# Blocks of 8 of a triangular inverse on VectorE, through DRAM there and back, in a hybrid recurrent layer

## The chip, the cores and the metric

One Trainium2 chip, one of its cores. The metric is the device time of one execution in microseconds (us), as the median of several runs. A core has TensorE (the page calls its products PE and its weight loads PEld), VectorE (DVE), ScalarE (ACT), GpSimd (POOL) and SyncE (SP), which here issues nearly all DMAs.

## What is computed

One layer that serves two groups of tokens: a prompt of 256 and eight sequences of 8 new tokens, 320 columns in all. In float32:

```python
h = rms_norm(x, norm_g)
p = einsum('nld,dp->nlp', h, w_in)          # one projection, 2048 -> 12416 columns
# branch A, 16 heads of 64: r, k, v, decay w, a from p (token shift, small LoRAs), kk = k normed
#   S_t = S_{t-1} diag(w_t) - (S_{t-1} kk_t)(kk_t * a_t)^T + v_t k_t^T ;  y_t = S_t r_t
# branch B, 8 heads of 128: a gated linear recurrence, S_t = diag(g_t) S_{t-1} + k_t v_t^T
merged = (sigmoid(p[..., OFF_GA:OFF_GB]) * (y_a @ proj_a)
          + sigmoid(p[..., OFF_GB:]) * (y_b @ proj_b))
y = x + merged @ w_out                      # then a last rms_norm; the states are outputs too
```

Branch A is computed in chunks of 64 tokens. Within a chunk the delta rule's update needs the inverse of a unit lower triangular matrix I + N of 64 x 64, one for each head and chunk, where N holds masked products of the keys. For the eight short sequences, N falls apart into blocks of 8.

## The kernel before, in words

All large products are made from float32r halves: each operand is split into a high part (a cast by ScalarE) and the rest (a subtraction by VectorE), and three products (high x high, high x low, low x high) are summed. hhi and hlo hold h, whi and wlo a block of 8 x 128 rows of weights, raw the loaded block (three buffers of each). One tile of 128 output columns takes 2 blocks, 48 products over 320 columns, in a PSUM tile mps.

Three stages:

- The start norms and transposes x, and makes the constants.
- The recorded stage. `record_all` writes down, for each of 8 head pairs p, the eight projection tiles r, k, v, za, q, f, i, zb, and then the recurrences `rwkv` (two heads of branch A) and `hgrn` (one head of branch B). After the pairs it records NFILL = 4 tiles of the gate ga. The calls go into a `Recorder`, which keeps each with an estimated cost and latency. `order()` plans all five engines with these: at each point it takes the operation whose inputs are due, by the longest path behind it, and fills TensorE with the projection's products (the "stream") where nothing else is due. The plan is then issued, so each engine's order is fixed, SP's too. Every instruction so issued has line 1447 in the profile. For operations that read another engine's result, TensorE's plan adds a margin of 250 ns. A DMA on SP is planned at 380 ns, and what needs it at 5500 ns more.
- The output stages. For each of 16 tiles m: the gates ga (made here unless m < NFILL) and gb, the products with proj_a and proj_b (ppa, ppb, lines 359 to 361), the merge (lines 1486 to 1494). Then the product with w_out (lines 1534 to 1540), and the last norm.

In `rwkv`, the part that the change touches runs like this. The masked products are in g2 (in the profile: g). nd (in the profile by its buffer, big) collects the prompt's N for the four chunks and two heads; TensorE transposes it, and ScalarE copies the result into M (buffer uE). The inverse Y is built by doubling: blocks of 2 are I - N by POOL and VectorE, from id64; then for sz = 2, 4, 8, 16, 32 the blocks of sz are joined to blocks of 2 sz by Y21 = -Y22 N21 Y11: a product with M (into a PSUM tile, pP), a masked copy into pp, a product with the transpose xt of Y (buffer uB; pD), and a subtraction into yz. yz holds Y with zeros between the two heads' halves, yd the same without; from the second level on yd is transposed by TensorE to make xt. ys is the inverse for the short sequences, which is done after sz = 4. Products of these operands are in plain float32, each as two instructions on TensorE.

The chain of a pair goes on from yz through four chunks (rhs, uv, st), the output y, a norm over heads (uE, uB), to ya, the pair's part of branch A's output. Most buffers are single: the exponential into uE of a pair follows the product into ya of the pair before.

Of the kernel before, what the change touches and what calls it, by code (L numbers as in the profile page):

```python
# [19 lines left out]
NT = NP_ + NS  # L20
# [18 lines left out]
EXP_LN_SET = 6  # L39

NFILL = 4
BUFS = {"r": 1, "k": 1, "v": 1, "za": 2, "q": 2, "f": 2, "i": 1, "zb": 1}


# [24 lines left out]
class Recorder:  # L69
# [15 lines left out]
    def add(self, eng, name, fn, args, kw):  # L85
# [8 lines left out]
        for j, x in enumerate(aps):  # L94
            t_ = x.tensor
            if "DRam" in type(t_).__name__:
                continue
            key = (t_.name, x.offset, tuple(map(tuple, x.ap)))
            if key not in self.spans:
                self.spans[key] = span_of(x)  # L100
            o.uses.append((*self.spans[key], j == 0, "PSUM" in str(x.space)))
# [193 lines left out]
def hybrid_step(ctx, tc, x_prompt, x_sample, state_rwkv, state_hgrn, state_shift, norm_g, w_in,  # L295
# [68 lines left out]
    def run(gen):  # L364
        for _ in gen:
            pass
# [9 lines left out]
    with tc.tile_pool(name="start", bufs=1) as st, \  # L376
# [53 lines left out]
        fetch(2, 0, 0)  # L430


        id64 = ctile([128, 64], "id64")
# [11 lines left out]
        lvs = st.tile([128, 5, 32], F32, name="lvs")  # L445
        lvz = ctile([128, 5, 2, 32], "lvz")
        seqm = ctile([128, NSEQ], "seqm")
        mk_lv = {}
        V.memset(lvs[low_], 1.0)
        G.memset(seqm[low_], 1.0)  # L450
        for n, sz in enumerate((2, 4, 8, 16, 32)):
            mk_lv[sz] = lvz[:, n]
            lv = lvs[low_, n].rearrange("p (b s) -> p b s", s=sz)
            nb = 32 // sz
            keep_ge(lv, [[-2 * sz, nb], [0, sz]], 0, 1)
            keep_ge(lv, [[2 * sz, nb], [0, sz]], sz - 1, -1)
# [267 lines left out]
             "w1": 384, "w2": 320, "w3": 320, "ks": 128, "ket": 256, "o": NT}  # L724


    CLEAR = {"uB", "uE", "ys", "rhs", "rhs2", "k3", "vm", "w1", "vt", "att", "attc", "az", "rz"}

    def at(name, shape=(128, NT), tag=None, bufs=1, dt=F32):
        tag = tag or name  # L730
# [48 lines left out]
    def rwkv(p, r, k, vp, za):  # L779
# [142 lines left out]
        two = lambda t_, x: t_.rearrange("p a (b two) -> p a b two", two=2)[:, :, :, x]  # L922
        two4 = lambda t_, x: t_.rearrange("p a h (b two) -> p a h b two", two=2)[:, :, :, :, x]
        ys = at("ys", (128, 2, 64))
        idx = [two(id64[:, None], j).to_broadcast([128, 5, 32]) for j in range(2)]
        V.tensor_mul(two(xt[:, 0:5], 0), two(xt[:, 0:5], 0), idx[1])
        V.tensor_sub(two(xt[:, 0:5], 0), idx[0], two(xt[:, 0:5], 0))
        G.tensor_copy(two(xt[:, 0:5], 1), idx[1])
        for c_ in range(2):
            y = yz[HS[c_], :, c_]  # L930
            src = two4(g2[HS[c_], c_:4:2, 0], 1)
            ix = [two(id64[HS[c_], None], j)[:, None].to_broadcast([64, 2, 2, 32]) for j in range(2)]
            G.tensor_mul(two4(y, 1), src, ix[0])
            G.tensor_sub(two4(y, 1), ix[1], two4(y, 1))
            G.tensor_copy(two4(y, 0), ix[0])
            G.tensor_copy(yd[HS[c_]], y)
        ix = [two(id64[0:64, None], j).to_broadcast([64, 2, 32]) for j in range(2)]
        G.tensor_mul(two(ys[0:64], 1), two(g2[0:64, 4, 0], 1), ix[0])
        G.tensor_sub(two(ys[0:64], 1), ix[1], two(ys[0:64], 1))
        G.tensor_copy(two(ys[0:64], 0), ix[0])  # L940


        bk = at("bk", (128, 5, 128))
# [8 lines left out]

        for sz in (2, 4, 8, 16, 32):
            smp = sz < 8
            if sz > 2:
                xt = at("xt", (128, 6, 64), tag="uB")
                px = aps("pX")
                for cp in range(2):  # L960
                    T.transpose(px[:, 128 * cp:128 * cp + 128], yd[:, cp].rearrange("p h t -> p (h t)"), ident)
                if smp:
                    T.transpose(px[:, 256:384], ys.rearrange("p h t -> p (h t)"), ident)
                n = 5 if smp else 4
                S.copy(xt[:, 0:n].rearrange("p c t -> p (c t)"), px[:, :64 * n])
            ahead = lambda t_: t_.rearrange("p (x two s) -> p x two s", two=2, s=sz)[:, :, 1, :]
            n = 5 if smp else 4
# [4 lines left out]
            if smp:  # L972
                T.matmul(ps[:, 256:320], M[:, 2].rearrange("p h t -> p (h t)"), ahead(ys.rearrange("p h t -> p (h t)")),
                         start=True, stop=True)
            pp = at("pp", (128, 5, 64))
            V.tensor_mul(pp[:, :n], ps[:, :64 * n].rearrange("p (c x) -> p c x", x=64),
                         mk_lv[sz].rearrange("p h t -> p (h t)")[:, None].to_broadcast([128, n, 64]))
# [4 lines left out]
            if smp:  # L982
                T.matmul(ps[:, 256:320], xt[:, 4:6, :].rearrange("p c t -> p (c t)"), pp[:, 4], start=True, stop=True)
# [6 lines left out]
            if smp:  # L990
                yv = ys[0:64].rearrange("p h (b two s) -> p (h b) two s", two=2, s=sz)[:, :, 1, :]
                V.tensor_sub(yv, yv, ps[0:64, 256:320].rearrange("p (x s) -> p x s", s=sz))

        bp = parts(bon)
        pbn = aps("pbn")
# [391 lines left out]
    def record_all():  # L1387
# [275 lines left out]
```

## Time and profile before

| | |
|---|---|
| runs | 1119.71, 1120.02, 1121.02 us; median 1120.02 |
| the profiled execution | span 1119.8 us; no other time of it is shown |
| TensorE busy | 1104.9 us, 9244 products |
| VectorE, ScalarE, GpSimd busy | 762.0, 694.2, 187.1 us |
| chain that ended last | TensorE 96% |
| recorded stage | 28.4 to 684.45 us |
| DMA | 159.89 MB, mean 143 GB/s |

Busy time counts an instruction from its start to its end. TensorE's instructions overlap, so a group's sum of lengths is longer than the time that it takes of TensorE; the time from one start to the next is what counts. "A <- B: x, n, y" in the waits says that A waited x us in total, n times, y at the longest, until B was done. Tiles go by their buffers' names: a stands for any PSUM tile of branch A, b for branch B's.

### The profile page before, as it was taken

What the parts mean: (1) busy time and instruction counts of PE and PEld (TensorE: products, weight loads), DVE (VectorE), ACT (ScalarE), POOL (GpSimd) and SP (SyncE); (2) the same over time, 40 slices, a digit from 0 to 9 for tenths busy, and PEclk for the clock granted to TensorE, in tenths of its full rate; (3) what the DMA queues carried; (4) which work ended last, traced back from release to release, by engine and by line L of the source; (5) the groups of instructions that cost most, each with busy time, mean ns of one, the idle gap of its engine ahead of it and who ended that gap; (6) DMA issues with size and microseconds to landing.
All of it is one profiled execution on the core that took longest, in us unless ns stands there. A gap on an engine that the chain in (4) does not pass through costs nothing.

```text
span 1119.8 us, 23680 instructions
## 1 busy us (share of the span) xinstructions
PE 1104.9 (99%) x9244; PEld 1068.4 (95%) x9244; DVE 762.0 (68%) x1631; ACT 694.2 (62%) x1578; POOL 187.1 (17%) x401
## 2 busy tenths in 40 slices
PE   7999999999999999999999999999999999999997
PEld 6999999999999999999999999999999999998886
DVE  8778888887888887887887876444444444437532
ACT  7677777777777778677776876444444444435422
POOL 7531231221311411412322200000000000000000
PEclk9999999999999999999999999999999999999999
DMA  6744545435436435445354345555555555586602
GB/s 193 194 125 117 153 116 148 138 99 155 123 91 165 127 102 165 134 114 156 113 136 133 107 136 148 146 147 152 149 148 152 149 152 150 151 274 227 201 32 95
DMA packets 283189, 159.89 MB, mean 143 GB/s; under 512 B 22909, under 2 KB 273280, under 8 KB 282500
## 3 DMA queue, kind: packets, MB, share of 16 engines
q1 hardware_dynamic: 282708, 157.06, 49.1%
q8 instruction: 73, 1.20, 0.5%
q10 hardware_dynamic: 368, 1.31, 0.3%
q14 instruction: 40, 0.33, 0.1%
HBM read 148.53 MB, written 9.81 MB: 141 GB/s over the span
## 4 chain that ended last, share of the span: by engine, by line
PE 96%; ACT 2%; DMA 1%; issue 0%; DVE 0%; SPq 0%; DVEq 0%; ACTq 0%
PE mps L1447 42%; PE a L1447 10%; PE mps L361 6%; PE mps L359 6%; PE mps L360 6%; PE b L1447 3%; PE po L1536 3%; PE po L1535 3%; PE po L1534 3%; PE ppb L359 2%; PE ppa L359 2%; PE ppa L361 2%; PE ppb L361 2%; PE ppb L360 2%; PE ppa L360 2%; PE y L1447 1%
## 5 line engine op out<-in xcount | busy, mean ns | idle before, releaser
L1447 PE MATMUL mps<-hhi,whi 128*128 128x320 f32 x1088 | 345.1, 317 | 0.0
L1447 PE MATMUL mps<-hlo,whi 128*128 128x320 f32 x1088 | 344.6, 317 | 0.0
L1447 PE MATMUL mps<-hhi,wlo 128*128 128x320 f32 x1088 | 344.0, 316 | 0.0
L1447 PEld LDWEIGHTS mps<-hhi,whi 128*128 128x128 f32 x1088 | 205.0, 188 | 3.6 <-issue 2.7
L1447 PEld LDWEIGHTS mps<-hlo,whi 128*128 128x128 f32 x1088 | 205.1, 189 | 1.1 <-issue 0.4
L1447 PEld LDWEIGHTS mps<-hhi,wlo 128*128 128x128 f32 x1088 | 205.0, 188 | 0.7
L349 ACT CAST whi<-raw 128x1024 fp32r<-128x1024 f32 x88 | 92.4, 1050 | 162.7 <-PE mps L360 107.3
L350 DVE TENSOR_TENSOR wlo<-raw,whi 128x1024 fp32r<-128x1024 f32 x88 | 107.9, 1226 | 125.0 <-ACT whi L349 124.8
L1447 DVE TENSOR_TENSOR wlo<-raw,whi 128x1024 fp32r<-128x1024 f32 x134 | 164.7, 1229 | 17.9 <-ACT whi L1447 16.7
L1447 ACT CAST whi<-raw 128x1024 fp32r<-128x1024 f32 x134 | 140.2, 1046 | 57.6 <-PE mps L1447 56.5
L361 PE MATMUL mps<-hhi,wlo 128*128 128x320 f32 x448 | 138.7, 310 | 0.0
L360 PE MATMUL mps<-hlo,whi 128*128 128x320 f32 x448 | 138.7, 309 | 0.0
L359 PE MATMUL mps<-hhi,whi 128*128 128x320 f32 x448 | 138.6, 309 | 0.0
L359 PEld LDWEIGHTS mps<-hhi,whi 128*128 128x128 f32 x448 | 84.1, 188 | 0.0
L360 PEld LDWEIGHTS mps<-hlo,whi 128*128 128x128 f32 x448 | 84.1, 188 | 0.0
L361 PEld LDWEIGHTS mps<-hhi,wlo 128*128 128x128 f32 x448 | 84.1, 188 | 0.0
L1523 DVE TENSOR_TENSOR wlo<-raw,whi 128x1024 fp32r<-128x1024 f32 x32 | 38.5, 1221 | 37.2 <-ACT whi L1522 36.9
L1522 ACT CAST whi<-raw 128x1024 fp32r<-128x1024 f32 x32 | 32.9, 1050 | 48.1 <-DMA raw<-in_w_out_dram 25.5
L1447 POOL TENSOR_TENSOR vm<-v,seq 96x512 fp32r<-96x512 f32 x16 | 16.8, 1051 | 200.2 <-ACT uK L1447 130.0
L1536 PE MATMUL po<-wlo,mhi 128*128 128x512 f32 x128 | 50.2, 392 | 0.0
L1535 PE MATMUL po<-whi,mlo 128*128 128x512 f32 x128 | 50.1, 391 | 0.0
L1534 PE MATMUL po<-whi,mhi 128*128 128x512 f32 x128 | 50.1, 391 | 0.0
(442 smaller groups left out, 2245.8 us busy)
## 6 DMA issues: line engine op xcount, KB each, us to landing
raw<-in_w_in_dram SPq DMA_DIRECT2D x194, 512.0 KB
raw<-in_w_out_dram SPq DMA_DIRECT2D x32, 512.0 KB
raw<-in_proj_a_dram SPq DMA_DIRECT2D x16, 512.0 KB
raw<-in_proj_b_dram SPq DMA_DIRECT2D x16, 512.0 KB
s<-in_state_hgrn_dram SPq DMA_DIRECT2D x8, 512.0 KB
out_dram<-s SPq DMA_DIRECT2D x8, 512.0 KB
s<-in_state_rwkv_dram SPq DMA_DIRECT2D x8, 256.0 KB
out_dram<-s SPq DMA_DIRECT2D x8, 256.0 KB
```

The costliest lines, as they stand in the source:

```text
L349: S.copy(hi[:, ks], raw[:, ks])
L350: sub.tensor_sub(lo[:, ks], raw[:, ks], hi[:, ks].bitcast(F32))
L359: T.matmul(dst, hi[:, q, :], xhi[:, k, :], start=(k == 0), stop=False)
L360: T.matmul(dst, hi[:, q, :], xlo[:, k, :], start=False, stop=False)
L361: T.matmul(dst, lo[:, q, :], xhi[:, k, :], start=False, stop=(k == nk - 1))
L1447: o.fn(*o.args, **o.kw)
L1522: S.copy(hi, raw)
L1523: V.tensor_sub(lo, raw, hi.bitcast(F32))
L1534: T.matmul(pt, h, hi, start=first, stop=False)
L1535: T.matmul(pt, l, hi, start=False, stop=False)
L1536: T.matmul(pt, h, lo, start=False, stop=end)
```

## The change

Levels 2 and 4 of the doubling go. The diagonal blocks of 8 x 8 of N (64 of the prompt's four chunks and two heads, 16 of the short sequences, and 16 of padding) are gathered into a tile dn (POOL masks, VectorE sums over the blocks of a row), written to a DRAM tile scratch[0] as 768 rows of 8 elements, and read back as nb with one block in each of 96 partitions. There VectorE makes their inverses in y8 by nine small operations: first the 2 x 2 corrections, then the 4 x 4 one. y8 goes to scratch[1] and comes back as ye in the first layout; POOL spreads it to yd and ys, and ScalarE copies yd into yz. All four DMAs are on SP. The planner takes 2600 ns for the latency of DMAs with these DRAM tiles.

Three more gate tiles (m = 4 to 6) are made at the end of the recorded stage, in free buffers of za, q and f; they are stored to DRAM and loaded again in the output loop.

```diff
+NLATE = 3
...
             if "DRam" in type(t_).__name__:
+                if t_.name.startswith("scr"):
+                    o.uses.append((t_.name, 0, 1, 1, j == 0, False))
                 continue
...
-            o.cost, o.lat = 380, 5500
+            o.cost, o.lat = 380, 2600 if any(u[0].startswith("scr") for u in o.uses) else 5500
...
+        id8 = ctile([128, 64], "id8")
+        G.memset(id8, 0.0)
+        G.memset(id8[:, 0:64:9], 1.0)
...
-        for n, sz in enumerate((2, 4, 8, 16, 32)):
+        for n, sz in enumerate((8, 16, 32)):
...
-        M = at("M", (128, 3, 2, 64), tag="uE")
+        M = at("M", (128, 2, 2, 64), tag="uE")
...
-        T.transpose(ps[:, 256:384], g2[:, 4, 0].rearrange("p h t -> p (h t)"), ident)
-        xt = at("xt", (128, 6, 64), tag="uB")
-        S.copy(xt[:, 0:5].rearrange("p c t -> p (c t)"), ps[:, :320])
         for h in range(2):
             for c_ in range(2):
-                S.copy(M[HS[c_], 0:2, h], xt[HS[h], c_:4:2])
-            S.copy(M[0:64, 2, h], xt[HS[h], 4])
+                S.copy(M[HS[c_], :, h], ps[HS[h], :256].rearrange("p (a c s) -> p a c s", c=2, s=64)[:, :, c_])
+
+        lows = at("lows", (128, 4, 8, 8), tag="pp")
+        each = lambda n: seqm[:, None, :, None].to_broadcast([128, n, 8, 8])
+        G.tensor_mul(lows, nd.rearrange("p a h (b j) -> p (a h) b j", j=8), each(4))
+        dn = at("dn", (128, 6, 8))
+        V.tensor_reduce(dn[:, 0:4], lows.rearrange("p c b j -> p c j b"), axis=mybir.AxisListType.X, op=ALU.add)
+        V.tensor_reduce(dn[0:64, 4:6], g2[0:64, 4, 0].rearrange("p h (b j) -> p h j b", j=8),
+                        axis=mybir.AxisListType.X, op=ALU.add)
+        there = lambda t_: t_.rearrange("(c p) j -> p c j", c=6)
+        whole = lambda t_: t_.rearrange("(q i) j -> q (i j)", i=8)
+        Y.dma_start(there(scratch[0]), dn)
+        nb = at("nb", (96, 64), tag="pp")
+        Y.dma_start(nb, whole(scratch[0]))
+        y8 = at("y8", (96, 64))
+        V.tensor_sub(y8, id8[:96], nb)
+        t8 = nb
+        four = lambda o_, *d: bass.AP(y8.tensor, y8.offset + o_, [y8.ap[0], *d])
+        t4 = t8[:, 0:4].rearrange("p (a i) -> p a i", i=2)
+        V.tensor_mul(t4, four(2, [36, 2], [8, 2]), four(19, [36, 2], [0, 2]))
+        V.tensor_add(four(3, [36, 2], [8, 2]), four(3, [36, 2], [8, 2]), t4)
+        V.tensor_mul(t4, four(10, [36, 2], [1, 2]), four(1, [36, 2], [0, 2]))
+        V.tensor_add(four(2, [36, 2], [1, 2]), four(2, [36, 2], [1, 2]), t4)
+        t64 = t8.rearrange("p (i j k) -> p i j k", j=4, k=4)
+        p16 = at("p16", (96, 4, 4))
+        V.tensor_mul(t64, four(4, [8, 4], [0, 4], [1, 4]), four(36, [0, 4], [1, 4], [8, 4]))
+        V.tensor_reduce(p16, t64, axis=mybir.AxisListType.X, op=ALU.add)
+        V.tensor_mul(t64, four(0, [8, 4], [0, 4], [1, 4]),
+                     p16.rearrange("p k j -> p j k")[:, None].to_broadcast([96, 4, 4, 4]))
+        V.tensor_reduce(four(4, [8, 4], [1, 4]), t64, axis=mybir.AxisListType.X, op=ALU.add)
+        Y.dma_start(whole(scratch[1]), y8)
+        ye = at("ye", (128, 6, 8))
+        Y.dma_start(ye, there(scratch[1]))
+
         ys = at("ys", (128, 2, 64))
-        idx = [two(id64[:, None], j).to_broadcast([128, 5, 32]) for j in range(2)]
-        V.tensor_mul(two(xt[:, 0:5], 0), two(xt[:, 0:5], 0), idx[1])
-        V.tensor_sub(two(xt[:, 0:5], 0), idx[0], two(xt[:, 0:5], 0))
-        G.tensor_copy(two(xt[:, 0:5], 1), idx[1])
...
+        wide = lambda t_: t_.rearrange("p h (b j) -> p h b j", j=8)
+        spread = lambda x, n: ye[x, 4 * (n == 2):4 * (n == 2) + n, None, :].to_broadcast([x.stop - x.start, n, 8, 8])
+        G.tensor_mul(yd.rearrange("p a h (b j) -> p (a h) b j", j=8), spread(slice(0, 128), 4), each(4))
+        G.tensor_mul(wide(ys[0:64]), spread(slice(0, 64), 2), each(2)[0:64])
         for c_ in range(2):
+            S.copy(yz[HS[c_], :, c_], yd[HS[c_]])
...
-        for sz in (2, 4, 8, 16, 32):
-            smp = sz < 8
-            if sz > 2:
+        for sz in (8, 16, 32):
...
             ps = aps("pP")
             for cp in range(2):
                 T.matmul(ps[:, 128 * cp:128 * cp + 128], M[:, cp].rearrange("p h t -> p (h t)"),
                          ahead(yz[:, cp].rearrange("p c h t -> p (c h t)")), start=True, stop=True)
-            if smp:
-                T.matmul(ps[:, 256:320], M[:, 2].rearrange("p h t -> p (h t)"), ahead(ys.rearrange("p h t -> p (h t)")),
-                         start=True, stop=True)
...
+    scr = ctx.enter_context(tc.tile_pool(name="scr", bufs=1, space=bass.MemoryType.DRAM))
+    scratch = [scr.tile([768, 8], F32, name=f"scr{j}", tag=f"scr{j}") for j in range(2)]
+    late = [scr.tile([128, NT], F32, name=f"scrg{m}", tag=f"scrg{m}") for m in range(NLATE)]
...
+        for m, (pool, key) in enumerate(((at, "za"), (bt, "q"), (bt, "f"))[:NLATE]):
+            def post(ps, m=m, pool=pool, key=key):
+                t_ = pool(key, (128, NT), bufs=BUFS[key])
+                sigm(t_, ps)
+                Y.dma_start(late[m], t_)
+            tile_of(OFF_GA + 128 * (NFILL + m), post)
...
             ga = fpr.tile([128, NT], F32, name="ga", tag="ga", bufs=2)
-            run(main(OFF_GA + 128 * m, lambda ps: sigm(ga, ps)))
+            if m < NFILL + NLATE:
+                nc.sync.dma_start(ga, late[m - NFILL])
+            else:
+                run(main(OFF_GA + 128 * m, lambda ps: sigm(ga, ps)))
```

More of the change, by code (lines that the diff above doesn't have):

```diff
@@ L430, in hybrid_step @@
         fetch(2, 0, 0)
-        id64 = ctile([128, 64], "id64")
+        id64 = st.tile([128, 64], F32, name="id64")
         G.tensor_add(id64, ident[:, 0:64], ident[:, 64:128])
@@ L444, in hybrid_step @@
         low_ = HS[0]
-        lvs = st.tile([128, 5, 32], F32, name="lvs")
-        lvz = ctile([128, 5, 2, 32], "lvz")
+        lvs = st.tile([128, 3, 32], F32, name="lvs")
+        lvz = ctile([128, 3, 2, 32], "lvz")
         seqm = ctile([128, NSEQ], "seqm")
@@ L724, in hybrid_step @@
              "w1": 384, "w2": 320, "w3": 320, "ks": 128, "ket": 256, "o": NT}
-    CLEAR = {"uB", "uE", "ys", "rhs", "rhs2", "k3", "vm", "w1", "vt", "att", "attc", "az", "rz"}
+    CLEAR = {"uB", "uE", "ys", "dn", "rhs", "rhs2", "k3", "vm", "w1", "vt", "att", "attc", "az", "rz"}
     def at(name, shape=(128, NT), tag=None, bufs=1, dt=F32):
@@ L923, in rwkv @@
-        two4 = lambda t_, x: t_.rearrange("p a h (b two) -> p a h b two", two=2)[:, :, :, :, x]
+                S.copy(M[HS[c_], :, h], ps[HS[h], :256].rearrange("p (a c s) -> p a c s", c=2, s=64)[:, :, c_])
[4 more added lines that the diff above has]
+        V.tensor_reduce(dn[:, 0:4], lows.rearrange("p c b j -> p c j b"), axis=mybir.AxisListType.X, op=ALU.add)
@@ L929, in rwkv @@
+        G.tensor_mul(yd.rearrange("p a h (b j) -> p (a h) b j", j=8), spread(slice(0, 128), 4), each(4))
+        G.tensor_mul(wide(ys[0:64]), spread(slice(0, 64), 2), each(2)[0:64])
         for c_ in range(2):
[L930 to L940, printed above, removed]
+            S.copy(yz[HS[c_], :, c_], yd[HS[c_]])
         bk = at("bk", (128, 5, 128))
@@ L950, in rwkv @@
         S.copy(bk[:, 4], ps[:, :128])
-        for sz in (2, 4, 8, 16, 32):
-            smp = sz < 8
-            if sz > 2:
[L958 to L961, printed above, removed]
-                if smp:
-                    T.transpose(px[:, 256:384], ys.rearrange("p h t -> p (h t)"), ident)
-                n = 5 if smp else 4
-                S.copy(xt[:, 0:n].rearrange("p c t -> p (c t)"), px[:, :64 * n])
+        for sz in (8, 16, 32):
+            xt = at("xt", (128, 4, 64), tag="uB")
+            px = aps("pX")
+            for cp in range(2):
+                T.transpose(px[:, 128 * cp:128 * cp + 128], yd[:, cp].rearrange("p h t -> p (h t)"), ident)
+            S.copy(xt.rearrange("p c t -> p (c t)"), px[:, :256])
             ahead = lambda t_: t_.rearrange("p (x two s) -> p x two s", two=2, s=sz)[:, :, 1, :]
-            n = 5 if smp else 4
             ps = aps("pP")
@@ L971, in rwkv @@
                          ahead(yz[:, cp].rearrange("p c h t -> p (c h t)")), start=True, stop=True)
-            if smp:
-                T.matmul(ps[:, 256:320], M[:, 2].rearrange("p h t -> p (h t)"), ahead(ys.rearrange("p h t -> p (h t)")),
-                         start=True, stop=True)
-            pp = at("pp", (128, 5, 64))
-            V.tensor_mul(pp[:, :n], ps[:, :64 * n].rearrange("p (c x) -> p c x", x=64),
-                         mk_lv[sz].rearrange("p h t -> p (h t)")[:, None].to_broadcast([128, n, 64]))
+            pp = at("pp", (128, 4, 64))
+            V.tensor_mul(pp, ps[:, :256].rearrange("p (c x) -> p c x", x=64),
+                         mk_lv[sz].rearrange("p h t -> p (h t)")[:, None].to_broadcast([128, 4, 64]))
             ps = aps("pD")
@@ L981, in rwkv @@
                          pp[:, 2 * cp:2 * cp + 2].rearrange("p c x -> p (c x)"), start=True, stop=True)
-            if smp:
-                T.matmul(ps[:, 256:320], xt[:, 4:6, :].rearrange("p c t -> p (c t)"), pp[:, 4], start=True, stop=True)
             for c_ in range(2):
@@ L989, in rwkv @@
                     S.copy(yd[HS[c_]].rearrange("p a h (b two s) -> p a (h b) two s", two=2, s=sz)[:, :, :, 1, :], y)
-            if smp:
-                yv = ys[0:64].rearrange("p h (b two s) -> p (h b) two s", two=2, s=sz)[:, :, 1, :]
-                V.tensor_sub(yv, yv, ps[0:64, 256:320].rearrange("p (x s) -> p x s", s=sz))
         bp = parts(bon)
```

1 line of the change is left out of this document (removed).

## The prediction

> **What bounds the kernel now.** I read the page's busy times first, then the stretches, then the waits. The first two lines of the fence are from the page, the next two from the stretches, cut where the recorded stage ends (684.45 us; columns: length, then the busy time of PE, PEld, DVE, ACT and POOL, granted clock, DMA share, GB/s); the last two are from the waits, with the total, the number and the longest.
>
> ```profile
> span 1119.8 us, 23680 instructions
> PE 1104.9 (99%) x9244; PEld 1068.4 (95%) x9244; DVE 762.0 (68%) x1631; ACT 694.2 (62%) x1578; POOL 187.1 (17%) x401
> 28.40:684.45 656.05, 655.22 (x6461) 641.20 (x6460) 540.59 (x1335) 489.08 (x1260) 165.46 (x353) 1.00 0.48 133
> 684.45:975.00 290.55, 290.55 (x1984) 290.55 (x1983) 131.49 (x160) 130.74 (x196) 0.00 (x0) 1.00 0.53 151
> PE a L1447 <- DVE pp L1447: 0.7, 2, 0.3
> ACT whi L1447 <- PE mps L1447: 56.5, 47, 2.7
> ```
>
> TensorE is never out of work: in the recorded stage it is busy for 655.2 of 656.1 us, at the full granted clock, and it waits 0.7 us there in all. So both stages last as long as TensorE's instructions. An instruction taken away saves the time from its start to the next start, if its place isn't taken by a wait. VectorE is busy for 82% of that stage (540.59 of 656.05), ScalarE for 75%.
>
> **What the change removes.** Per head pair, TensorE loses the third transpose into M, all of levels 2 and 4 (three products, three corrections each), and level 4's three transposes back. Pair 2's timeline of TensorE has them (start, length, how many). Lengths overlap, so I take starts.
>
> ```profile
> 225.64 0.38 PE L1447 MATMUL a<-ident,big 128*128 128x128 f32 x2
> 225.85 0.27 PE L1447 MATMUL a<-ident,g 128*128 128x128 f32 x1
> 225.88 0.39 PE L1447 MATMUL mps<-hhi,wlo 128*128 128x320 f32 x1
> 226.11 0.31 PE L1447 MATMUL mps<-hhi,whi 128*128 128x320 f32 x1
> 226.26 0.31 PE L1447 MATMUL mps<-hlo,whi 128*128 128x320 f32 x1
> ...
> 228.72 0.61 PE L1447 MATMUL a<-yz,uE 128*128 128x128 f32 x4
> 229.09 0.39 PE L1447 MATMUL mps<-hhi,wlo 128*128 128x320 f32 x1
> 229.32 0.33 PE L1447 MATMUL a<-ys,uE 128*128 128x64 f32 x2
> 229.46 0.39 PE L1447 MATMUL mps<-hhi,whi 128*128 128x320 f32 x1
> 229.69 0.31 PE L1447 MATMUL mps<-hlo,whi 128*128 128x320 f32 x1
> ...
> 236.76 0.78 PE L1447 MATMUL a<-pp,uB 128*128 128x128 f32 x6
> 237.35 0.39 PE L1447 MATMUL mps<-hlo,whi 128*128 128x320 f32 x1
> 237.58 0.31 PE L1447 MATMUL mps<-hhi,wlo 128*128 128x320 f32 x1
> ...
> 238.61 0.61 PE L1447 MATMUL a<-yz,uE 128*128 128x128 f32 x4
> ```
>
> A stream product (mps) takes 0.147 us from start to start (226.11 to 226.26, rounded). Three transposes: 226.11 - 225.64 - 0.147 = 0.32, or 0.11 each. A level's products: 229.69 - 228.72 less two stream products = 0.68. Its corrections: 237.58 - 236.76 - 0.147 = 0.67. Per pair: 0.11 + 2 x (0.68 + 0.67) + 3 x 0.11 = 3.14 us. Eight pairs: **25.1 us**.
>
> **What it moves.** Three gate tiles of 48 products go from the output stage into the recorded one. Two rows of the output loop's multiply by the gate, of tiles whose gate is made before it and of the others (first and last start at the end), give the price:
>
> ```profile
> L1486 DVE TENSOR_TENSOR mt<-ga,ppa x12: 486/489/489, 758.4 to 990.7; 128x320 f32<-128x320 f32 x12
> L1486 DVE TENSOR_TENSOR mt<-sga,ppa x4: 487/489/489, 695.0 to 737.3; 128x320 f32<-128x320 f32 x4
> ```
>
> (990.7 - 758.4) / 11 = 21.1 us against (737.3 - 695.0) / 3 = 14.1: a gate tile is 7.0 us of TensorE, 48 x 0.147, in either stage. Sum 0: 21.1 leave one stage and enter the other. Their three stores and three loads of 160 KB stand on SP; the loads ahead of the gb weights, three blocks before TensorE needs those, so I cost them at 0. The cover is that prefetch: without it, a late weight block would show in the output loop as a TensorE wait, of which the second stretch has none. ScalarE's nine exponentials and logarithms move along with the tiles, into ScalarE's free quarter.
>
> **What it adds.** No TensorE work, but a longer chain from the masked products g to the third level: copies, a POOL product and two VectorE sums, four DMAs that each wait for the one before or for VectorE, nine small VectorE operations, a POOL product, two ScalarE copies. Prices from the groups by shape (count | busy us, mean ns), and from ScalarE's timeline (first row):
>
> ```profile
> 224.47 0.82 ACT L1447 COPY big<-g 64x256 f32<-64x256 f32 x2
> L1447 POOL TENSOR_TENSOR fd<-id,fq 128x256 fp32r<-128x256 f32 x16 | 12.1, 758 | 7.6 <-DVE fq L1447 5.1 <-PE a L1447 2.2
> L1447 DVE TENSOR_TENSOR pp<-a,lvz 128x256 f32<-128x256 f32 x24 | 10.2, 425 | 2.6 <-PE a L1447 2.2
> L1447 DVE TENSOR_TENSOR rhs<-a,uK 64x64 f32<-64x64 f32 x48 | 10.6, 221 | 3.8 <-PE a L1447 3.1
> L1447 DVE TENSOR_TENSOR fq<-f,fh 32x8 fp32r<-32x8 f32 x32 | 8.3, 260 | 0.7
> ```
>
> Copies 0.82 + POOL 0.76 + two sums at 0.43 + subtraction 0.22 + four tiny ones at 0.26 + four of 64 elements at 0.22 + POOL 0.76 + copies 0.82 = 6.2 us, and four trips. VectorE's part is 3.0 us a pair, and it loses ten operations, two of them 128x320 products and two over xt, so I count it as no busier; its free 18% covers an error there. POOL loses twelve operations a pair and gains three.
>
> A trip has no row of its own. Its bounds are two cases of 32 KB. The first two rows are stretches around a store issued at 506.87 (SP's row follows): the DMA engines are idle until 508.10 and move it by 508.60, so a trip is not under 1.7 us. The last four are weights of 32 KB that queue behind 512 KB loads at the start: SP issues them, and the casts that wait for them (the releaser is in brackets) start 41.43 - 36.09 = 5.3 and 42.42 - 37.83 = 4.6 us later.
>
> ```profile
> 506.80:508.10 1.30, 1.30 (x12) 1.30 (x11) 0.45 (x2) 0.85 (x4) 0.00 (x0) 1.00 0.00 1
> 508.10:508.60 0.50, 0.50 (x8) 0.50 (x6) 0.21 (x2) 0.50 (x3) 0.00 (x0) 1.00 0.31 66
> 506.87 0.65 SPq L1447 DMA_DIRECT2D out_dram<-so  x1
> 36.09 1.64 SPq L1447 DMA_DIRECT2D w2a<-in_rwkv_w_dram  x1
> 37.83 0.55 SPq L1447 DMA_DIRECT2D w2a<-in_rwkv_a_dram  x1
> 41.43 0.30 ACT L1447 CAST wst<-w2a 64x128 fp32r<-64x128 f32 x1 [0.16 <-DMA w2a<-in_rwkv_w_dram]
> 42.42 0.30 ACT L1447 CAST ast<-w2a 64x128 fp32r<-64x128 f32 x1 [0.69 <-DMA w2a<-in_rwkv_a_dram]
> ```
>
> The DMA engines are 0.48 busy in this stage, so about half of the trips meet a load. At 1.7 us for one half and midway to 4.6 (3.2) for the other, plus 0.3 for the completion (my estimate), a trip is 2.7 us; I take the low end's neighbourhood since a trip issues while SP holds the following loads back. The order written out by the planner counts 0.38 + 2.6 = 2.98. That is what matters: every engine runs the planner's order, so a trip that lands earlier gains nothing, and one that lands later holds TensorE at the third level's product, past the 0.25 us that the planner leaves, and holds behind it the stream and, on SP, the weight loads. SP's own hold is hidden: ScalarE's casts wait for TensorE to free buffers (56.5 us, 47 times), not for loads. A quarter of the trips would meet the first half of a load and land up to 4.6 - 2.98 = 1.6 us late. I count that as one late trip of the four in a pair, by 0.7 us, less 0.25: 0.45 x 8 = **3.6 us**.
>
> The Trainium skill's page "DMA: Bandwidth & Descriptors" (section "Anatomy of one DMA") gives about 2.0 us fixed for one DMA issued by GpSimd, most of it the receipt of the write. The idle 1.3 us in the row above, ahead of any data, says that here much of it lies before the data. By the page no trip would exceed the plan, and the sum would be 1094.7.
>
> **Is the chain too long?** Pair after pair, the exponential into uE waits for the product into ya of the pair before. Their rows (first and last start) and the last piece of the chain that ended last before the stage's end:
>
> ```profile
> L1447 ACT ACTIVATE uE<-uB x8: 456/458/476, 44.1 to 603.2; 128x320 f32<-128x320 f32 x8
> L1447 DVE TENSOR_TENSOR ya<-uE,uA x8: 476/483/493, 128.2 to 677.3; 128x320 f32<-128x320 f32 x8
> 674.63 9.82 PE mps L1447 x67
> ```
>
> The last pair takes 677.3 - 603.2 = 74.1 us. From the copies at 224.47 to the third level at 238.61 are 14.1 us now; 6.2 + 4 x 2.98 = 18.1 after, so a chain is 78.1. TensorE's pace is (677.3 - 128.2) / 7 = 78.4 now and 75.3 after. The chain falls behind by 2.8 us a pair, 22 over eight. It has 684.45 - 677.8 (the last ya's end) = 6.7 us to spare, and the three gate tiles add 21.1 of work that doesn't need it: 27.8. So the lag is hidden. The tiles matter for this alone; without them some 16 us would come back as a wait.
>
> **Sum.** 1119.8 - 25.1 + 0 + 3.6 = 1098.3. The profiled execution's span is 0.2 under the median of the runs shown (1120.02), so the forecast is **1098.5 us**.
>
> **Rivals.**
> 1. Trips late throughout. With landings of 3.2 to 3.7 us, each of 32 costs 0.2 to 0.7 over the plan: 1119.8 - 25.1 + 6 to 22 = 1101 to 1117, middle 1109. For it: the 4.6 and 5.3 above. Against: those stood behind three 512 KB loads.
> 2. Slower: the same place, TensorE's wait at the third level, from 2.98 + 25.1 / 32 = 3.76 us a trip on. At 4.6 it is 32 x 1.62 = 52 us lost, 1146. For it: SP is one queue in order, and the weights' packets stand ahead of the small ones. Against: 0.48 busy, not 1.
> 3. The 32-byte rows. The first store and the last load of a pair move 768 rows each. The 32 KB store's 128 rows pass within the 0.5 us stretch. If rows set the time, 768 take up to 6 x 0.5 = 3.0 us, and such a trip up to 1.3 + 3.0 + 0.3 = 4.6, 1.6 over the plan; at half of that, for two trips a pair, 16 x 0.8 = 13 us, 1108. The same page ("Specifications") says that a transfer under 512 B costs a read and a write back. No row here shows one of 32 B; that would act on the store alone, 8 x 0.8 = 6 us, 1101.
> 4. Nothing comes of it: freed TensorE time turns into waits of the same length, trips of 3.7 to 3.8 us, 1118 to 1122.
>
> **How the numbers follow.** Chances: the forecast (1092 to 1104) 0.52, rival 1 0.15, rival 3 0.09 (0.03 of it by the page's rule, at 1101), rival 4 0.06, slower 0.18. Faster by over 0.2% (2.2 us, what a measurement can tell) is 0.76, same 0.06, slower 0.18. The range, from the sum without any wait, less 2.5 for slots measured in one pair, past rival 1's end: 1092 to 1119; it leaves out the slower cases and most of rival 4.
>
> **What would show it.** Right: the pairs' pace between ya products at 75 to 76 us; TensorE's waits in the stage at 3 to 8 us, most for yz or yd by way of POOL, ScalarE or a DMA; the stage ending near 681; ya of the last pair before it; tiles 4 to 6 of the output loop 14.1 us apart. Wrong: waits over 20 us behind DMAs into nb or ye, SP's longest waits there, a pace of 78 or more, or an idle TensorE at the stage's end.

## The result, and the profile after

The changed kernel takes **1105.1 us** (median; 1102.3 to 1106.5) against 1120.2 us for the kernel before in the same session: a ratio of 0.986, 95% interval 0.9846 to 0.9874. The forecast was 1098.5 us in a range of 1092 to 1119. So it is faster, as forecast, by 15.1 us instead of 21.5.

The profiled execution of the changed kernel took 1104.5 us with a span of 1102.8: some 1.7 us lie outside a span. The span of 1119.8 shown for the kernel before therefore belongs to an execution of about 1121.5, a little above its median, and the two spans overstate the gain by some 1.9 us. That 1119.8 came out near the median, from which the forecast was counted, is chance. In this part the recorded stage's line is 1465 (1447 before, a few lines off in the kernels of the experiments), and the output loop's product with the gate is line 1507 (1486 before). The page of the changed kernel:

```profile
span 1102.8 us, 23134 instructions
PE 1081.3 (98%) x9020; PEld 1043.5 (95%) x9020; DVE 750.6 (68%) x1639; ACT 680.1 (62%) x1530; POOL 154.6 (14%) x328
```

TensorE lost 23.6 us of busy time, near the 25.1 forecast, but its idle time, span less busy, rose from 14.9 to 21.5 us. Where that lies is seen in the stretches (length, then the busy time of PE, PEld, DVE, ACT and POOL, the granted clock, DMA share, GB/s) and in TensorE's waits (total, number, longest):

```profile
28.40:683.95 655.55, 650.01 (x6363) 635.32 (x6362) 529.88 (x1336) 476.71 (x1209) 135.96 (x281) 1.00 0.50 139
...
691.95:695.00 3.05, 1.78 (x8) 1.02 (x8) 2.37 (x4) 2.88 (x5) 0.00 (x0) 1.00 0.89 266
695.00:698.40 3.40, 3.40 (x16) 3.40 (x15) 2.61 (x5) 2.95 (x7) 0.00 (x0) 0.52 0.56 161
```

```profile
PE b L1465 <- issue: 1.9, 1, 1.9
...
PE a L1465 <- DVE yz L1465: 1.2, 2, 0.6
PE a L1465 <- POOL yd L1465: 1.0, 1, 1.0
PE mps L362 <- ACT whi L352: 1.0, 1, 1.0
PE a L1465 <- ACT uv L1465: 0.5, 1, 0.5
PE mps L1465 <- ACT pad L1465: 0.5, 1, 0.5
PE a L1465 <- issue: 0.4, 1, 0.4
...
PE mps L364 <- DVE wlo L353: 0.2, 1, 0.2
```

The waits in the stage and at its end add up to 6.7 us where there were 0.7. Only 2.2 us of them are behind the new inverse (yz and yd), and only the 1.0 us for yd, in pair 2, is behind a trip: the two waits for yz are for VectorE's subtraction, at later levels of the doubling. Most of the idle time lies inside the stage: in the first stretch TensorE is idle for 5.5 us, where the kernel before has 0.8. The second stretch is the stage's end: TensorE has 8 products to start in 3 us, and in the next 3.4 us the granted clock is 0.52. The products stand 0.27 us apart there instead of 0.147, which costs some 1.5 us more (13 products by 0.12).

The chain's own pace, from the groups of the tiles uE, ya and mt (first and last start at the end):

```profile
L1465 ACT ACTIVATE uE<-uB x8: 455/460/475, 42.5 to 612.6; 128x320 f32<-128x320 f32 x8
```

```profile
L1465 DVE TENSOR_TENSOR ya<-uE,uA x8: 465/488/494, 130.5 to 692.1; 128x320 f32<-128x320 f32 x8
```

```profile
L1507 DVE TENSOR_TENSOR mt<-ga,ppa x12: 486/489/490, 755.7 to 974.0; 128x320 f32<-128x320 f32 x12
L1507 DVE TENSOR_TENSOR mt<-sga,ppa x4: 482/488/490, 701.1 to 741.6; 128x320 f32<-128x320 f32 x4
```

From ya to ya a pair takes (692.1 - 130.5) / 7 = 80.2 us; it was 78.4 before, and the forecast's chain was 78.1. The last ya stands at 692.1 instead of 677.3. The output loop is as foreseen: from the first tile with ga to the last, 218.3 us are two steps of 14.1 and nine of 21.1.

**Why the chain is longer than its parts.** Pair 2, in order: ScalarE's copies, SP's four DMAs, VectorE's nine small operations (with two of the casts that stand between them), POOL's product, TensorE's first transpose and the third level's first product.

```profile
223.81 0.82 ACT L1465 COPY big<-g 64x256 f32<-64x256 f32 x2
```

```profile
227.49 0.41 SPq L1465 DMA_DIRECT2D scr<-dn  x1
231.42 0.33 SPq L1465 DMA_DIRECT2D pp<-scr  x1
239.35 0.33 SPq L1465 DMA_DIRECT2D scr<-y  x1
242.36 0.37 SPq L1465 DMA_DIRECT2D ye<-scr  x1
```

```profile
233.14 0.22 DVE L1465 TENSOR_TENSOR y<-id,pp 96x64 f32<-96x64 f32 x1
...
233.49 0.15 DVE L1465 TENSOR_TENSOR pp<-y 96x4 f32<-96x4 f32 x1
...
233.96 1.22 DVE L1465 TENSOR_TENSOR wlo<-raw,whi 128x1024 fp32r<-128x1024 f32 x1
235.09 0.15 DVE L1465 TENSOR_TENSOR y<-y,pp 96x4 f32<-96x4 f32 x1
...
235.37 0.15 DVE L1465 TENSOR_TENSOR pp<-y 96x4 f32<-96x4 f32 x1
...
235.76 0.15 DVE L1465 TENSOR_TENSOR y<-y,pp 96x4 f32<-96x4 f32 x1
...
236.04 0.27 DVE L1465 TENSOR_TENSOR pp<-y 96x64 f32<-96x64 f32 x1
...
236.69 1.23 DVE L1465 TENSOR_TENSOR wlo<-raw,whi 128x1024 fp32r<-128x1024 f32 x1 [0.18 <-ACT whi L1465]
237.84 0.21 DVE L1465 TENSOR_REDUCE p<-pp 96x16 f32<-96x64 f32 x1
...
238.72 0.26 DVE L1465 TENSOR_TENSOR pp<-y,p 96x64 f32<-96x64 f32 x1
...
239.12 0.21 DVE L1465 TENSOR_REDUCE y<-pp 96x16 f32<-96x64 f32 x1
```

```profile
247.22 1.25 POOL L1465 TENSOR_TENSOR yd<-ye,seqm 128x256 f32<-128x256 f32 x1 [2.35 <-DMA ye<-scr]
```

```profile
248.52 0.44 PE L1465 MATMUL a<-ident,yd 128*128 128x128 f32 x2 [1.04 <-POOL yd L1465]
...
249.53 0.61 PE L1465 MATMUL a<-yz,uE 128*128 128x128 f32 x4
```

The nine operations are 1.77 us of work. They take 6.2 us, from 233.14 to the store's issue at 239.35, since each waits for the one before and VectorE does other work in between: of the 6.2 us it is busy for 5.5. Where no cast stands between two steps, the next one starts 0.28 to 0.40 us later, once 0.88; where one does, 1.6 and 1.8 us later. Over the eight pairs VectorE is busy for 4.95 of 5.82 us, and 1.8 of that are the nine operations. Against the forecast's parts (us):

| from ... to | forecast | measured mean |
|---|---|---|
| copies of g ... first store | 2.44 | 3.15 |
| four trips, each to the next start | 11.92 | 2.84 + 3.11 + 3.22 + 3.15 = 12.32 |
| nine small operations | 2.14 | 5.82 |
| POOL's product ... third level | 1.58 | 2.70 |
| sum | 18.1 | 24.0 |

On average the trips were priced right within 0.1 us; single ones took 1.7 to 4.9 us to the next start, and 18 of the 32 more than the plan's 2.98. Work that was priced by its busy time was not: 6.2 us forecast, 11.7 measured. The pair lost less than that, since from the last yz to ya it now takes 30.4 us instead of 35.5.

### The profile page after: what moved, and what is told of

Read it like the earlier page. It is cut to its first block, busy times and chain, and to the rows that moved or that the text cites. A ratio compares the mean times of both kernels' runs of the same rounds, so it can differ in the third digit from the quotient of the medians.

```text
span 1102.8 us, 23134 instructions
## 1 busy us (share of the span) xinstructions
PE 1081.3 (98%) x9020; PEld 1043.5 (95%) x9020; DVE 750.6 (68%) x1639; ACT 680.1 (62%) x1530; POOL 154.6 (14%) x328
## 4 chain that ended last, share of the span: by engine, by line
PE 95%; ACT 2%; DMA 1%; DVE 1%; issue 0%; POOL 0%; DVEq 0%; SPq 0%; ACTq 0%
PE mps L1465 45%; PE a L1465 9%; PE mps L362 5%; PE mps L364 5%; PE mps L363 5%; PE b L1465 3%; PE po L1555 3%; PE po L1556 3%; PE po L1557 3%; PE ppa L363 2%; PE ppa L364 2%; PE ppa L362 2%; PE ppb L362 2%; PE ppb L363 2%; PE ppb L364 2%; PE y L1465 1%
## 5 line engine op out<-in xcount | busy, mean ns | idle before, releaser
L363 PEld LDWEIGHTS mps<-hlo,whi 128*128 128x128 f32 x400 | 75.2, 188 | 0.0
L1543 ACT CAST whi<-raw 128x1024 fp32r<-128x1024 f32 x32 | 33.1, 1052 | 47.7 <-PE po L1560 21.1
L362 PE MATMUL ppa<-yah,whi 128*128 128x320 f32 x128 | 40.1, 314 | 0.1
```

The lines of the kernel that those rows point to most:

```text
L362: T.matmul(dst, hi[:, q, :], xhi[:, k, :], start=(k == 0), stop=False)
L363: T.matmul(dst, hi[:, q, :], xlo[:, k, :], start=False, stop=False)
L1543: S.copy(hi, raw)
```

## The experiments

The theory after the comparison, Q: the chain of a pair is longer than forecast because its added steps run one by one between VectorE's other work, its lag outgrows the cover, and TensorE waits for it around the stage's end. The rival, R: trips that land later than planned hold TensorE inside the stage, as the prediction had it. They differ in what more cover, a shorter chain and another planned length of a trip would do.

Times are medians; each ratio is to the kernel before on the same chip, with its 95% interval.

| kernel | us | ratio | ya to ya, us |
|---|---|---|---|
| the changed kernel | 1105.1 | 0.986 (0.9846 to 0.9874) | 80.2 |
| e1 blocks alone | 1112.1 | 0.9929 (0.9911 to 0.9948) | 79.9 |
| e2 tiles alone | 1121.9 | 1.0016 (1.0006 to 1.0025) | 78.5 |
| e3 five tiles | 1099.5 | 0.9815 (0.98 to 0.9829) | 80.7 |
| e4 no trips | 1097.3 | 0.9795 (0.9781 to 0.981) | 75.2 |
| e5 small operations on POOL | 1096.4 | 0.9787 (0.9772 to 0.9801) | 79.2 |
| e6 small operations first | 1102.5 | 0.9843 (0.9826 to 0.9859) | 79.5 |
| e7 trips planned at 1.7 | 1114.6 | 0.9949 (0.9935 to 0.9964) | 81.2 |
| e8 POOL and five tiles | 1100.9 | 0.9829 (0.9814 to 0.9844) | 80.6 |
| e9 POOL, no tiles | 1110.7 | 0.992 (0.9903 to 0.9936) | 78.6 |
| e10 trips planned at 4.0 | 1131.6 | 1.0105 (1.009 to 1.012) | 83.9 |
| e11 five of the nine | 1098.9 | 0.9807 (0.9791 to 0.9824) | 79.8 |
| e12 four beside the chain | 1098.3 | 0.9805 (0.9791 to 0.982) | 79.3 |

**The two halves of the change, apart.**

```
- NLATE = 3
+ NLATE = 0
```

> The changed kernel with no gate tile moved (NLATE = 0): the inverse's blocks of 8 alone. The prediction's theory (the chain falls behind by 22 us, the stage has 6.7 to spare, and the three tiles hide the rest): about 16 us come back, 1114 us. Theory Q (VectorE places its nine small operations among the weights' casts, a chain of 80 us a pair, the stage ends on the chain): the last ya stays near 692 us, as in the changed kernel, and the output loop is as long as before, 1118 to 1122 us. Rival R (only trips that land later than planned cost time, the chain's length does not matter): 1105 us, as with the tiles.

It took 1112.1, 7.0 more than with the tiles: the prediction's 1114 was nearer than theory Q's 1118 to 1122. The last ya is at 684.3, not at 692. TensorE also made 42 more gate products of the output stage, 6.2 us, ahead of its first product into ppa than in the changed kernel (3404 stream products against 3506 less the three tiles' 144). So the output loop itself may cover a part of a late chain, which theory Q left out; that is argued, not shown.

```
  (the kernel before)
+ NLATE = 3, the three stores and the three loads
```

> The kernel before with the three gate tiles moved into the recorded stage, stored and loaded again, and the old inverse. The prediction's theory and Q: the sum is 0, 1120 us within 2, output tiles 4 to 6 spaced 14.1 us, last ya near 677. A rival by which the tiles themselves save time (a late load of a gb weight block or the exponentials at the output loop): 1113 us or less. The store and load cost something: over 1122.

It took 1.8 us more than the kernel before (0.7 to 2.8 by the interval). Output tiles 4 to 6 are 14.1 us apart and the last ya is at 676.1, so the move itself is the exchange of 21.1 for 21.1 that was forecast. The profiled span is 1119.8, as before, but the kernel before's profile is of a longer execution than its median, with a granted clock of 0.94 in the first 28.4 us against 1.00 here. TensorE's idle time is 16.6 us instead of 14.9, and 0.7 of it are waits that the kernel before doesn't have, for the casts of ya at the first products into ppa:

```profile
PE ppa L363 <- DVE yal L1481: 0.4, 1, 0.4
...
PE ppa L362 <- ACT yah L1480: 0.3, 1, 0.3
```

The rest of the 1.8 us is not followed up.

**More cover, and no trips.**

```
- NLATE = 3 ... ((at, "za"), (bt, "q"), (bt, "f"))[:NLATE]
+ NLATE = 5 ... ((at, "za"), (bt, "q"), (bt, "f"), (at, "za"), (bt, "q"))[:NLATE]
```

> The changed kernel with five gate tiles moved instead of three. Prediction's theory (the lag is hidden already by three, what is lost is lost to late trips inside the stage): 1103 to 1107 us, no change. Theory Q (the chain ends the stage, TensorE idles and then runs at a lower clock there): 14 us more of work stand ahead of the last ya, the idle places between 688 and 696 us and the slow clock behind them go, 1098 to 1101 us.

1099.5: in theory Q's range. The chain did not become shorter (80.7 us a pair, last ya at 695.7); two more tiles of work that needs nothing of it took 5.6 us off the time. But the gain doesn't lie where theory Q had it:

```profile
28.40:683.95 655.55, 654.15 (x6315) 640.83 (x6314) 531.22 (x1336) 480.13 (x1213) 144.63 (x281) 1.00 0.51 140
...
699.90:703.40 3.50, 2.11 (x12) 1.47 (x11) 1.61 (x2) 2.45 (x4) 0.00 (x0) 1.00 0.96 282
703.40:706.80 3.40, 3.40 (x15) 3.40 (x14) 2.61 (x5) 3.28 (x7) 0.00 (x0) 0.50 0.77 232
```

At the stage's end TensorE still idles for 1.4 us and then runs at half the clock. What went are waits inside the stage: 1.4 us of idle time in the first stretch instead of 5.5. Why more work at the end takes away waits in the middle is not shown; the planner made another order of the whole stage.

```
- Y.dma_start(there(scratch[0]), dn); Y.dma_start(nb, whole(scratch[0]))
- V.tensor_sub(y8, id8[:96], nb)
+ V.tensor_sub(y8, id8[:96], <the sums in dn, read in place>)
- Y.dma_start(whole(scratch[1]), y8); Y.dma_start(ye, there(scratch[1]))
+ ye = y8's own tile
```

> The changed kernel without its four scratch DMAs a pair: the subtraction reads the sums in dn directly, and ye is a view of the small operations' own tile, so the inverse's values are not those of the reference and only the time counts. Prediction's theory and Q alike: the chain loses 4 trips of 2.6 to 2.7 us a pair and no longer ends the stage, the gaps go, 1095 to 1098 us, last ya under 665. If TensorE's lost 25 us were overestimated, or something else than the chain costs the time, it stays over 1101.

1097.3 us. This kernel leaves out the exchange between partitions, so its inverse is another matrix. The group of ya, without trips:

```profile
L1462 DVE TENSOR_TENSOR ya<-uE,uA x8: 481/482/486, 128.9 to 655.3; 128x320 f32<-128x320 f32 x8
```

(655.3 - 128.9) / 7 = 75.2 us a pair is the pace of TensorE's own work; the forecast had 75.3 for it. With the tiles' 1.8 us taken out, the blocks are worth 1120.05 + 1.8 - 1097.3 = 24.6 us to TensorE, where the forecast had 25.1. In the changed kernel the trips and what they stretch cost 1105.1 - 1097.3 = 7.8 us.

**The nine small operations.**

```
- V.tensor_sub(y8, id8[:96], nb) ... and eight more on V
+ G.tensor_sub(y8, id8[:96], nb) ... and eight more on G, each sum over four as two additions
```

> The changed kernel with three tiles, and the nine small VectorE operations between the two pairs of DMAs issued by POOL instead (each of the two sums over four written as two additions, eleven operations). The trips stay. Theory Q (the small operations wait for their turn among VectorE's casts): from the issue of the load into nb to the issue of the store from y8 falls from 8 us to 5 to 6, the last ya comes before 688, 1098 to 1101 us. Rival R (late trips cost the time, wherever the operations run): 1104 to 1106 us, waits of TensorE in the stage as in the changed kernel. If POOL's operations take longer than the wait on VectorE: over 1106.

1096.4 us, 8.7 less than the changed kernel, and by disjoint intervals faster than both kernels of the case. The last ya (684.5) came as theory Q said; the time is 1.6 us under its range, and its reason, a shorter part between the load and the store, did not come. POOL's timeline of pair 2 has the first and the last of the eleven operations, and between them the shortest and the longest:

```profile
232.52 0.48 POOL L1467 TENSOR_TENSOR y<-id,pp 96x64 f32<-96x64 f32 x1 [0.78 <-DMA pp<-scr]
...
233.89 0.20 POOL L1467 TENSOR_TENSOR pp<-y 96x4 f32<-96x4 f32 x1
...
235.02 1.30 POOL L1467 TENSOR_TENSOR pp<-pp 96x32 f32<-96x32 f32 x1
...
237.46 0.35 POOL L1467 TENSOR_TENSOR y<-pp 96x16 f32<-96x16 f32 x1
```

From the first one's start to the store's issue it is 6.1 us on average (5.8 on VectorE), and from the load's issue to the store's 9.1 (8.9). That part did not shrink. Others did: from the copies to the first store 2.5 us instead of 3.15, from that store's issue to the load's 2.5 instead of 2.8, from POOL's product to the third level 2.05 instead of 2.70. The pair came out 1.0 us shorter. TensorE's wait in the stage is 1.0 us, three times behind yd, and no other is listed after the start of the kernel.

```
+ if o.first: return 4, o.rank      # in the planner's choice; set for the nine operations
```

> The changed kernel with three tiles, and the nine small operations chosen by the planner ahead of anything else that VectorE has ready, the weights' casts too. Theory Q: the chain loses some 2 to 4 us a pair, and the casts have the slack for it: 1099 to 1102 us. Rival R: 1104 to 1106 us. If the casts have no slack for it, TensorE waits for wlo, over 1106.

1102.5, between theory Q's range and R's; the ratio's interval overlaps that of the changed kernel. The nine operations stand first in VectorE's queue of choices, and their part still takes 5.5 us. The edit did not put the other work out from between them: VectorE is busy for 4.98 of these 5.53 us, with 1.6 casts a pair (1.75 in the changed kernel), since whatever is ready while the next step isn't still goes ahead. So a step costs its place in that order, and not its own 0.15 to 0.27 us. The next two kernels, run last, take up the number of steps. Theory Q' in them is Q with this reason.

```
- four of the nine operations, those behind the subtraction (blocks of 2 into blocks of 4)
```

> The changed kernel with three tiles, on VectorE, without the first four of the nine small operations (blocks of 4 are then not merged, so only the time counts). In the changed kernel nine steps take 5.8 us from the first one's start to the store's issue, so four fewer are some 2.6 us a pair. Theory Q' (the number of steps that wait for one another sets the chain, and the chain's lag over the cover is the loss): 1096 to 1100 us. If the steps do not matter: 1104 to 1106 us.

```
- the same four
+ four of that size on V, on a tile of zeros of their own, recorded after the store
```

> The same four taken out of the chain, and four of the same kind and size put on VectorE beside it, on a tile of zeros that nothing reads, so that VectorE's work stays as it is in the changed kernel. Theory Q' (steps in series): as without them, 1096 to 1100 us. Rival V (what helped when POOL took the operations over was VectorE's relief, not a shorter chain): 1103 to 1107 us.

1098.9 and 1098.3. Both kernels leave out the joining of blocks of 2. The part falls from 5.8 to 3.4 us in both, and the time by 6 to 7 us in both, though in the second VectorE does as much as in the changed kernel. So fewer steps in the chain help without any relief of VectorE, and rival V's 1103 to 1107 is out. A step taken out is worth 0.6 us of the part, 0.15 of them its own. It does not follow that relief did nothing in e5, where the part is no shorter and the time fell further. Why the neighbouring parts became shorter there stays open: in e12 they are as short (2.5, 2.6 and 2.25 us) with the operations on VectorE, and the planner made another order of the whole stage in each.

**The planned length of a trip.**

```
- o.lat = 2600 for a scratch DMA
+ o.lat = 1700      (e7)
+ o.lat = 4000      (e10)
```

> The changed kernel with the trips planned at 0.38 + 1.7 us instead of 0.38 + 2.6, nothing else. By the landings in the changed kernel's trace (1.6 to 4.8 us, mean 2.7) most trips then land later than planned. The prediction's theory (every engine runs the planner's order, so a late trip holds TensorE at the third level's product): 32 trips late by some 0.9 us, 15 to 25 us of TensorE waits behind yd and yz, 1113 to 1123 us. Theory Q (the chain's length counts, and the order has room for late trips): waits under 8 us, and the earlier place of the chain in VectorE's order helps, 1098 to 1104 us.

> The changed kernel with the trips planned at 0.38 + 4.0 us instead of 0.38 + 2.6, nothing else. The prediction's theory (a trip that lands earlier than the plan gains nothing, since every engine runs the planned order): the order is made for a chain that is 5.6 us longer a pair, 1120 to 1137 us, few waits behind yd. If the landings alone set the time: 1100 to 1106 us, as few trips come late.

1114.6 and 1131.6, both in the ranges of the prediction's theory. With 1.7, TensorE's first wait in the list is the one behind the inverse:

```profile
PE a L1465 <- POOL yd L1465: 9.6, 8, 2.7
```

That is the place that the theory named, with less than the 15 to 25 us of waits expected there. The time rose by 9.5 us.

With 4.0 the waits behind yd fall to 0.6 us, and TensorE stands elsewhere:

```profile
PE mps L1465 <- ACT pad L1465: 17.5, 6, 6.2
```

The trips did not become longer. From the load's issue to the first small operation it is 6.0 us instead of 3.1, since the order puts that operation later. The stream, which the planner lets run meanwhile, comes to a tile whose products wait for ScalarE's copy into pad. Behind such waits the granted clock is about 0.5 in five stretches, 24 us in all, and TensorE is busy for 1089.3 us instead of 1081.3. That kernel is slower than the one before the change. One number of the planner is worth 26 us here.

**Both remedies, and the cover again.**

```
  e5 + NLATE = 5      (e8)
  e5 + NLATE = 0      (e9)
```

> Both: the small operations on POOL and five tiles moved. Theory Q: nothing of the chain is left to hide, so it is no better than the kernel without the DMAs (1097.3 us) and no worse than five tiles alone (1099.5 us): 1097 to 1100 us. If POOL's operations cost time, over 1100.

> The small operations on POOL, no gate tile moved. The prediction's theory, that the tiles matter as cover alone and some 16 us come back without them: 1096.4 less the 1.8 that the tiles cost by themselves plus 16, 1110 us. Theory Q with the chain that POOL leaves (78 to 79 us a pair, last ya near 680): 1107 to 1111 us. Rival: with the shorter chain no cover is needed: 1094 to 1097 us.

1100.9 and 1110.7. Two more tiles on top of POOL bring nothing; it is 4.5 us worse than e5, more than the tiles' own 0.6 each, and over theory Q's range. That difference was not followed up. Each of these kernels has an order of its own, so some 4 us between two of them can come without any of the causes named here, and a difference of that size does not show one. Without tiles (e9) the time rises by 14.3 us, 16.1 with their own 1.8: the prediction's "some 16 us", though beside the changed kernel itself (e1) it is 7.0, 8.8 with the 1.8.

## Why the prediction was right, and where its sizes were off

**TensorE's 25.1 us**: 24.6 by e4 and e2, and the pace of TensorE's work 75.2 instead of 75.3. Right.

**The tiles, sum 0**: 1.8 us too little. 0.7 of it shows as waits for the casts of ya (e2); that the loads and stores, costed at 0, cost the rest isn't shown.

**Late trips, 3.6 us**: the mechanism is right (e7: late trips hold TensorE behind yd; e10: early ones gain nothing), the size too large. At the planned 2.98 us, against a mean of 3.08 to the next engine's start, TensorE waited 1.0 us behind yd, once. So 18 of 32 trips over the plan cost less than the one in four that was counted.

**The chain is hidden**: this is the step that failed. "6.2 + 4 x 2.98 = 18.1" took the added operations by their busy time. They are steps in series with other work of their engines between them, and stood at 24.0. The lag was put at 2.8 us a pair over eight, 22, under a cover of 27.8. Measured against e4's pace it is 80.2 - 75.2 = 5.0 us over seven steps from the first ya, 35. The same count for the others (cover 6.7 + 7.0 a tile; loss: the time above 1097.3 + 0.6 for each tile more or less than three):

| kernel | lag, us | cover | lag beyond it | measured loss |
|---|---|---|---|---|
| changed | 35 | 27.8 | 7 | 7.8 |
| e3 | 39 | 41.9 | 0 | 1.0 |
| e5 | 28 | 27.8 | 0 | -0.9 |
| e12 | 29 | 27.8 | 1 | 1.0 |
| e11 | 32 | 27.8 | 4 | 1.6 |
| e6 | 30 | 27.8 | 2 | 5.2 |
| e9 | 24 | 6.7 | 17 | 15.2 |
| e1 | 33 | 6.7 | 26 | 16.6 |
| e8 | 38 | 41.9 | 0 | 2.4 |
| e7 | 42 | 27.8 | 14 | 17.3 |
| e10 | 61 | 27.8 | 33 | 34.3 |

The count holds within some 3 us except in e1, which lost 9 us less than it says. The 6.2 us of output work that e1 does early don't explain this, since e9 does the same 3404 products early and fits. It is a rough count: a wait of TensorE inside the stage lengthens the lag as well as the time, so the two columns are not independent, and where the waits fall it does not say. In the changed kernel and in e3 the traces have most of the difference inside the stage and not at its end. What the experiments show is that trips and steps taken out, and cover added, bring 5.6 to 7.8 us back; that the lag over the cover is how they do so is argued. Rival R's times, 1103 to 1107 for e3 and 1104 to 1106 for e5 and e6, did not come.

The miss of 6.6 us is thus, rounded, 0.5 (TensorE) + 1.8 (tiles) + 4.2 (7.8 lost, by trips and chain together, instead of 3.6).

**The signs to watch.** TensorE's waits in the stage were to be 3 to 8 us, most of them for yz or yd: they are 6.7, of which a third is for yz or yd. The last ya was to stand before the stage's end near 681: it is at 692.1, the stage's last product starts at 689.0, and TensorE's idling there was named as a sign of being wrong, like a pace of 78 or more, which is 80.2. The pace of 75 to 76 us was a slip of the prediction itself: by its own working the chain sets the pace of ya, 78.1, and TensorE's 75.3 only the cover's use.

**The rivals.** Late trips throughout (1101 to 1117) holds the measured time, but not by its cause: with 18 of 32 trips over the plan, TensorE waited behind them for 1.0 us in all. The mean of 3.08 is far from the 3.76 us from which the slower case decides. That the 32-byte rows set the time is out, by the first pair of the changed kernel (first starts at the end):

```profile
L1465 SPq DMA_DIRECT2D scr<-dn x8: 366/367/423, 66.5 to 627.5; - x8
L1465 SPq DMA_DIRECT2D pp<-scr x8: 328/330/1520, 68.5 to 631.3; - x8
```

The store of 768 rows of 32 bytes lets the load behind it go after 68.5 - 66.5 = 2.0 us. On average this store took 2.84 us and the one of 96 rows 3.22. The 0.3 us for a trip's completion, which no row ahead of the result showed, agrees: 2.0 against the 1.7 until the data had moved. The Trainium skill's page "DMA: Bandwidth & Descriptors" (section "Specifications") has a read and a write back for transfers under 512 bytes; no cost of it is to be seen here. Its 2.0 us of fixed cost for a DMA issued by GpSimd ("Anatomy of one DMA") agrees with this trip on SP, during which the DMA engines were 0.19 busy, and not with the mean of 3.08 in a stage where they are half busy. Rival 4, that nothing comes of the change, is out: of TensorE's 24.6 us, 7.8 came back as lost time and 16.8 stayed.

## What to carry to other kernels

Price an added chain by its steps, not by the sum of its busy times: nine operations of 0.15 to 0.27 us in series took 5.8 us on a VectorE that put 3.2 us of other work between them, and four fewer gave 6 to 7 us of the kernel. Where a chain runs beside a stream that needs nothing of it, write down the lag over all its rounds and the work that stands behind it at the stage's end; in most of these kernels the time lost was near what is over that work. In an order written out ahead, the planned length of a transfer should be the measured one: too short by 0.9 us cost 9.5 us, and too long by 1.4 cost 26.5.

## What the runs showed of the hardware

POOL did these small operations at 0.20 to 0.48 us each in the pair shown, apart from one of 1.30; VectorE took 0.15 to 0.27. On average POOL's eleven are 4.9 of the 6.1 us that their part takes, VectorE's nine 1.8 of 5.8: the parts are alike for different reasons, slower steps on the one and other work between them on the other.

A short pause can have an aftermath: behind 3 us in which TensorE was busy for 1.78, the granted clock was 0.52 for the 3.4 us of the stretch shown above, and behind 3.5 us with 2.11 busy it was 0.50 for as long (e3). It need not: in e6 (689 to 693 us) TensorE was busy for 2.00 of 4.0 us and in e7 (407 to 411.3) for 1.62 of 4.3, and the granted clock behind was 1.00. The Trainium skill's page "TensorE: Matmul & The Clock Gate" (section "Part 1: The HAM clock gate") has half the clock after an idle window of some 3.4 us and the full one after a busy window; the length of the slow stretch agrees, but the stretch ahead of it was not idle throughout. What tells the two cases apart is not shown.
